# Strassen's seven products for the two down projections of a hybrid decoder layer

## The chip, the cores and the metric

One NeuronCore of one Trainium2 chip runs the whole layer in one launch. The metric is device time in microseconds, the median of several executions. In profiles, PE is TensorE's matmul, PEld its weight load, DVE is VectorE, ACT is ScalarE, POOL is GpSimd, and SP is the engine whose queue issues the DMAs.

## The reference

The kernel computes one decoder layer in float32 over 1024 tokens and 1024 channels. The change touches the two feed-forward blocks:

```python
def swiglu(x, w_gate, w_up, w_down):
    return (jax.nn.silu(x @ w_gate) * (x @ w_up)) @ w_down

x = x + 0.5 * swiglu(rmsnorm(x, ffn1_norm), ffn1_w_gate, ffn1_w_up, ffn1_w_down)   # D_FF = 2816
h = rmsnorm(x, mix_norm)
x = x + hybrid_mixer(h, ...)      # attention branch, delta-rule branch, gates, output projection
x = x + 0.5 * swiglu(rmsnorm(x, ffn2_norm), ffn2_w_gate, ffn2_w_up, ffn2_w_down)
return rmsnorm(x, final_norm)
```

The gate and up weights are 1024 x 2816, the down weights 2816 x 1024. The 2816 features are 22 tiles of 128.

## The kernel before

**Number format.** A float32 operand is split into two parts that TensorE takes at full rate: H, the value cast on ACT, and L, the rest, subtracted on DVE. A product of two split operands takes three matmuls (H·H, H·L, L·H). Weights and streamed operands come by DMA into a raw buffer (`wraw`, 128 x 1024), are cast into `wH` and subtracted into `wL` (`load_w2`, L204 and L205). `Weights` hands raw buffers and H/L pairs out in turn from several pools.

**Order.** The program is written as a sequence of tile operations. When the kernel is built, a planner gives every engine and the DMA queue a fixed order: among the instructions whose inputs and buffers it counts as ready it takes the one that stands first in the program, so that later work can be put ahead of earlier work that still waits. On the chip each queue then runs strictly in that order.

**Gate and up** (`hidden_tiles`). The features are worked on in 11 pairs of tiles, j = 0 to 10. For each j the gate half and the up half are each computed by Strassen's seven products: the input is cut into token halves and channel halves (blocks `B11`, `B21`, `T1` to `T4`, `B22`, made once and kept in SBUF), the weights into feature tile and channel halves (`seven_weights`, four POOL sums into `wS`, L346, and casts, L354 and L355). A half is 7 x 12 = 84 matmuls. The results arrive through PSUM in `ev`, `sg` and `su`. `gate_up` multiplies silu(gate) by up on POOL (L423) and stores each 128 x 512 piece to DRAM (`hd`, L424). For j = 0 and 1 (`EARLY`) two of the seven products are done earlier, while the last inputs are being made.

**Down** (`down`). Four chunks of 6, 6, 6 and 4 feature tiles; in each chunk hidden tiles (`hidH`, `hidL`, eight buffers each) and weights are loaded and split, and for every token tile t (8 of 128) and column half nh (2 of 512) one PSUM bank sums over the chunk with the hidden tile as the stationary operand (L537). DVE then adds half of the bank to x in SBUF (L539). x is loaded at the head (L552). The last chunk goes token tile by token tile, with `done(t)` after each: in the first feed-forward block the normalization of the mixer's input, in the second the final norm and the store of the output.

**Buffers.** The first feed-forward block has four raw buffers and five H/L pairs (`wp` with three, `wp1` with two), the second four raw buffers and four pairs in gate and up. `gB` is a single buffer for a gain vector, used by `load_gain`.

Of the kernel before, what the change touches and what calls it, by code (L numbers as in the profile page):

```python
# [9 lines left out]
F32 = mybir.dt.float32  # L10
# [6 lines left out]
P = 128  # L17
# [46 lines left out]
class Weights:  # L64
# [25 lines left out]
def psum(C, tag):  # L90
    return C.pp.tile([P, 512], F32, name=tag, tag=tag, bufs=BANKS[tag])
# [148 lines left out]
def load_gain(C, g):  # L240
    gB = C.tp.tile([P, D], F32, name="gB", tag="gB", bufs=1)
    C.nc.sync.dma_start(gB, bass.AP(tensor=g.tensor, offset=g.offset, ap=[[0, P], [1, D]]))
    return gB
# [177 lines left out]
def gate_up(C, out, sg, hd, i, a, eng=None):  # L421

    (eng or C.nc.gpsimd).tensor_tensor(out=out, in0=out, in1=sg, op=ALU.mult)  # L423
    C.nc.sync.dma_start(hd[:, i, a * 512:a * 512 + 512], out)  # L424


EARLY = 2
# [54 lines left out]
    return banks  # L482


def hidden_tiles(C, XB, wg, wu, hd, banks, whole):

    nc = C.nc

    def tiles(tag, bufs):
        return [[C.fp.tile([P, 512], F32, name=tag, tag=tag, bufs=bufs) for _ in range(2)] for _ in range(2)]  # L490

    for j in range(DFF // P // 2):
        rest = ((1, 1), (1, 0), (0, 1)) if j < EARLY else ((0, 0), (1, 1), (1, 0), (0, 1))

        def half(w, tag, bufs):
            early = banks.pop(0) if j < EARLY else None
            out = tiles(tag, bufs) if whole else None
            W = seven_weights(C, w, j * 256, early is not None)
            out = out or tiles(tag, bufs)
            first = j == 0 and w is wg and not whole  # L500
            seven_products(C, W, XB, out, early, PIECES if first else WHOLE, "tC" if first else "tA")
            return out

        g = half(wg, "sg", 5)
        for i, a in rest:
            nc.scalar.activation(g[i][a], g[i][a], AF.Silu)
        u = half(wu, "su", 4)
        for i, a in rest:
            gate_up(C, u[i][a], g[i][a], hd[j], i, a)


def down(C, tc, x, src, wd, hd, chunks, last, done, side):

    nc = C.nc

    def hidden(f0, n, a):
        tiles = []
        for j in range(f0 // 2, (f0 + n) // 2):
            to = [C.fp.tile([P, SLOT], F32R, name=t, tag=t, bufs=8 if not C.last else 4) for t in ("hidH", "hidL")]
            H, L = load_w2(C, hd[j][:, :, a * 512:a * 512 + 512], 2, 512, to)  # L520
            tiles += [(H[:, i], L[:, i]) for i in range(2)]
        return tiles

    def wtiles(f0, n, nh):
        W = []
        for k2 in range(0, n, 2):
            r = (f0 + k2) * P
            H, L = load_w2(C, wd[r:r + 256, nh * 512:nh * 512 + 512].rearrange("(k p) n -> p k n", p=P), 2, 512)
            W += [(H[:, 0], L[:, 0]), (H[:, 1], L[:, 1])]
        return W  # L530

    def one(t, nh, hid, W):
        ps = psum(C, "tC" if nh else "mm")
        m = slice(t % 4 * P, t % 4 * P + P)
        seq = [(hid[t // 4][k][i], W[k][w]) for k in range(len(W)) for i, w in ((0, 0), (0, 1), (1, 0))]
        for i, (h, w) in enumerate(seq):
            nc.tensor.matmul(ps, h[:, m], w, start=i == 0, stop=i == len(seq) - 1)  # L537
        xs = x[t][:, nh * 512:nh * 512 + 512]
        nc.vector.scalar_tensor_tensor(xs, ps, 0.5, xs, op0=ALU.mult, op1=ALU.add)  # L539

    f0 = 0
    C.last = False
    with tc.tile_pool(name="hid", bufs=1, side=side, reuse_waits="tile") as C.fp:
        for n in chunks:
            hid = []
            for nh in (0, 1):
                W = wtiles(f0, n, nh)
                for t in range(NT):
                    if nh == 0 and t % 4 == 0:
                        hid.append(hidden(f0, n, t // 4))  # L550
                    if f0 == nh == 0:
                        nc.sync.dma_start(x[t], src[t * P:t * P + P])  # L552
                    one(t, nh, hid, W)
            f0 += n
    C.last = True
    with tc.tile_pool(name="hidl", bufs=1, side=side, reuse_waits="tile") as C.fp:
        last()
        Ws = [wtiles(f0, 4, 0), wtiles(f0, 4, 1)]
        hid = [hidden(f0, 4, a) for a in (0, 1)]
        for t in range(NT):  # L560
            for nh in (0, 1):
                one(t, nh, hid, Ws[nh])
            done(t)

# [926 lines left out]
def ffn2(C, tc, I, out, hs):  # L1491

    nc = C.nc
    wg, wu = I["ffn2_w_gate"], I["ffn2_w_up"]
    C.XB = {}
    for i, names in enumerate((("B11", "B21"), ("T2", "T1"))):
        for q, n in enumerate(names):
            C.XB[n] = [b[i][:, q * 4:q * 4 + 4, :] for b in (C.hH, C.hL)]
    with ExitStack() as st:
        x2p = st.enter_context(tc.tile_pool(name="x2", bufs=1, side="right"))  # L1500

        x2 = dict((t, x2p.tile([P, D], F32, name=f"x2{t}")) for t in (0, 4, 1, 5, 2, 6, 3, 7))
        late, W2 = merge_out(C, tc, I, x2)
        with tc.tile_pool(name="xb2", bufs=1, reuse_waits="tile") as xb:
            for n in ("T3", "B22", "T4"):
                C.XB[n] = [xb.tile([P, 4, 512], F32R, name=n + h) for h in "HL"]
            with tc.tile_pool(name="lo", bufs=1) as lo:
                banks = early_products(C, I, late, W2, lo)
            st.close()
            with tc.tile_pool(name="f2", bufs=1, reuse_waits="tile") as C.fp:  # L1510
                C.wp.add(C.tp, 2, 0, "xs")
                hidden_tiles(C, C.XB, wg, wu, C.hd, banks, True)
    hs.close()
    with tc.tile_pool(name="x3", bufs=1, reuse_waits="tile") as xp:
        C.wp.add(xp, 0, 2)
        x = [xp.tile([P, D], F32, name=f"x{t}") for t in range(NT)]

        def done(t):
            y = xp.tile([P, D], F32, name="y", tag="xg", bufs=3)
            nc.gpsimd.tensor_tensor(out=y, in0=x[t], in1=C.gF, op=ALU.mult)  # L1520
            r = rstd(C, x[t], xp)
            nc.scalar.activation(y[:, :512], y[:, :512], AF.Copy, scale=r)  # L1522
            nc.sync.dma_start(out[t * P:t * P + P, :512], y[:, :512])
            nc.vector.tensor_scalar(y[:, 512:], y[:, 512:], r, None, op0=ALU.mult)  # L1524
            nc.sync.dma_start(out[t * P:t * P + P, 512:], y[:, 512:])

        def last():
            C.gF = load_gain(C, I["final_norm"])

        down(C, tc, x, C.x2d, I["ffn2_w_down"], C.hd, (6, 6, 6), last, done, "right")  # L1530


def layer(tc, I, out):
# [4 lines left out]
    with ExitStack() as st, ExitStack() as hs:  # L1538
# [17 lines left out]
        C.hd = [C.dp.tile([P, 2, T], F32, name=f"hd{j}") for j in range(DFF // P // 2)]  # L1556
        C.hH, C.hL = [None, None], [None, None]

        def open_h(a):
# [12 lines left out]
def ffn1(C, tc, I, open_h):  # L1572

    nc = C.nc
    with ExitStack() as st:
        C.wp.add(st.enter_context(tc.tile_pool(name="wp1", bufs=1)), 2, 2)
        C.tp = st.enter_context(tc.tile_pool(name="tp1", bufs=1))
        consts(C, I)
        with tc.tile_pool(name="xb", bufs=1) as xb:
            XB = {n: [xb.tile([P, 4, 512], F32R, name=n + h) for h in "HL"] for n in XBLOCKS if n != "T4"}  # L1580
            wg, wu = I["ffn1_w_gate"], I["ffn1_w_up"]
            with tc.tile_pool(name="s1", bufs=1) as sp:
                banks = early_tiles(C, tc, XB, I, wg, wu, C.hd, sp)
            with tc.tile_pool(name="f1", bufs=1, reuse_waits="tile") as C.fp:
                hidden_tiles(C, XB, wg, wu, C.hd, banks, False)
# [4 lines left out]
        with tc.tile_pool(name="x1", bufs=1, reuse_waits="tile") as xp:  # L1590
            x = []
            for t in range(NT):
                x.append(xp.tile([P, D], F32, name=f"x{t}"))
# [12 lines left out]
                if t > 1:  # L1606
                    late.pop(0)()

            down(C, tc, x, I["x"], I["ffn1_w_down"], C.hd, (6, 6, 6), lambda: open_h(1), done1, "left")

            C.begun = {}
            for c0, (H, L), at in ((C_QA, W[0], None), (C_KA, W[1], {5: late[1]})):
# [30 lines left out]
```

## Time and profile before

| | |
|---|---|
| median of 3 runs | 2669.09 us (2668.16 to 2672.79) |
| the profiled execution: its own time | 2673.94 us |
| its span in the trace | 2672.2 us |
| PE busy | 2581.1 us, 97%, 13007 matmuls |
| DVE busy | 1463.4 us, 55% |
| ACT busy | 1032.2 us, 39% |
| POOL busy | 468.3 us, 18% |
| DMA | 262.12 MB, mean 98 GB/s |
| granted TensorE clock, mean | 0.99 |

Busy time of PE is of pipelined matmuls, so that a stretch with 100% says that matmuls follow each other, not how long one occupies the array; the number of matmuls in a stretch says that. In the rows, the left tile is what is written, the right ones what is read; "x443" is a count; the text behind an arrow names what ended the idle time of the engine. The first feed-forward block spans about 0 to 710 us (its down from 471), the mixer to about 1980, the second block to the end (its down from about 2412).

### The profile page before, as it was taken

Reading aid. Unit: us, or ns where it says so; the run is one execution under the profiler, and the core shown is the slowest. Engines: PE = TensorE matmul, PEld = TensorE weight load, DVE = VectorE, ACT = ScalarE, POOL = GpSimd, SP = SyncE. Lnnn points to the kernel's source line nnn. Section 1 sums busy time; section 2 is a strip of 40 time slices with the busy share of each in tenths; the row PEclk is TensorE's granted clock in tenths of the full one; section 3 lists DMA queues with packets and bytes.
Section 4 is the critical chain, followed back from the end, with each engine's and each line's share of the span. In section 5 each row is a group of like instructions: output and inputs, shape, how many; then the busy total and the mean of one; then the engine's idle time right before and its main releaser. Section 6 shows DMA issues by size and latency. Waiting matters only on the chain. (4 is left out here: it accounts for less than half of the span.)

```text
span 2672.2 us, 34694 instructions
## 1 busy us (share of the span) xinstructions
PE 2581.1 (97%) x13007; PEld 2138.7 (80%) x13007; DVE 1463.4 (55%) x3276; ACT 1032.2 (39%) x1738; POOL 468.3 (18%) x378
## 2 busy tenths in 40 slices
PE   6999999999999999999999999999999999999997
PEld 5888888788788788787788888877877888887886
DVE  6444444432743547868867878445764444444326
ACT  5333333211544338445454444344433333332113
POOL 5534442000200000000000000000004445430002
PEclk9999999999999999999999999999999999999999
DMA  5323223531331222223222222367533232226311
GB/s 151 90 88 89 81 76 97 199 101 58 112 99 51 74 74 55 62 68 90 78 62 62 60 59 72 121 204 241 182 99 104 79 90 87 80 83 216 102 57 71
DMA packets 298809, 262.12 MB, mean 98 GB/s; under 512 B 39856, under 2 KB 232592, under 8 KB 298640
## 3 DMA queue, kind: packets, MB, share of 16 engines
q1 hardware_dynamic: 298640, 259.90, 31.9%
q8 instruction: 102, 1.67, 0.3%
q14 instruction: 67, 0.55, 0.1%
HBM read 195.26 MB, written 58.29 MB: 95 GB/s over the span
## 5 line engine op out<-in xcount | busy, mean ns | idle before, releaser
L229 PE MATMUL mm<-hH,wL 128*128 128x512 f32 x1072 | 442.0, 412 | 0.1
L229 PE MATMUL mm<-hL,wH 128*128 128x512 f32 x1072 | 419.8, 392 | 0.0
L229 PE MATMUL mm<-hH,wH 128*128 128x512 f32 x1072 | 418.9, 391 | 0.0
L204 ACT CAST wH<-wraw 128x1024 fp32r<-128x1024 f32 (+1 forms) x138 | 143.7, 1045 | 300.8 <-PE mm L537 123.8
L229 PEld LDWEIGHTS mm<-hL,wH 128*128 128x128 f32 x1072 | 201.5, 188 | 45.7
L229 PEld LDWEIGHTS mm<-hH,wL 128*128 128x128 f32 x1072 | 202.2, 189 | 43.7 <-issue 5.3
L205 DVE TENSOR_TENSOR wL<-wraw,wH 128x1024 fp32r<-128x1024 f32 (+1 forms) x138 | 169.7, 1231 | 112.8 <-ACT wH L204 105.6
L229 PEld LDWEIGHTS mm<-hH,wH 128*128 128x128 f32 x1072 | 202.5, 189 | 35.1
L355 DVE TENSOR_TENSOR wL<-wS,wH 128x1024 fp32r<-128x1024 f32 x88 | 126.8, 1441 | 162.1 <-ACT wH L354 161.3
L346 POOL TENSOR_TENSOR wS<-wraw 128x512 f32<-128x512 f32 x66 | 84.1, 1295 | 563.9 <-PE tA L296 322.8
L423 POOL TENSOR_TENSOR su<-su,sg 128x512 f32<-128x512 f32 x84 | 133.3, 1598 | 185.8 <-DVE su L397 161.6
L354 ACT CAST wH<-wS 128x1024 fp32r<-128x1024 f32 x88 | 92.5, 1053 | 151.0 <-PE tC L365 110.0
L393 ACT COPY ev<-mm 128x512 f32<-128x512 f32 (+1 forms) x118 | 68.5, 581 | 201.7 <-PE mm L365 201.7
L537 PE MATMUL mm<-wH,hidH 128*128 128x512 f32 x352 | 137.8, 392 | 3.0 <-DVE x L539 1.9
L537 PE MATMUL mm<-wH,hidL 128*128 128x512 f32 x352 | 137.5, 391 | 2.6 <-DVE hidL L205 2.6
L537 PE MATMUL tC<-wH,hidH 128*128 128x512 f32 x352 | 137.4, 391 | 1.9 <-ACT wH L204 1.9
L537 PE MATMUL mm<-wL,hidH 128*128 128x512 f32 x352 | 137.1, 390 | 1.3 <-DVE wL L205 1.3
L537 PE MATMUL tC<-wL,hidH 128*128 128x512 f32 x352 | 137.6, 391 | 0.5 <-DVE wL L205 0.5
L537 PE MATMUL tC<-wH,hidL 128*128 128x512 f32 x352 | 137.7, 391 | 0.0
L914 POOL MEMSET xp<- 128x3 f32 x24 | 2.4, 100 | 653.9 <-PE tA L775 250.9
L539 DVE SCALAR_TENSOR_TENSOR x<-mm,x 128x512 f32<-128x512 f32 x64 | 44.0, 689 | 105.2 <-PE mm L537 104.3
L539 DVE SCALAR_TENSOR_TENSOR x<-tC,x 128x512 f32<-128x512 f32 x64 | 44.0, 688 | 86.6 <-PE tC L537 86.5
(432 smaller groups left out, 6029.0 us busy)
## 6 DMA issues: line engine op xcount, KB each, us to landing
wraw<-in_w_in_dram SPq DMA_DIRECT2D x64, 512.0 KB, 4.1
wraw<-in_ffn_w_gate_dram SPq DMA_DIRECT2D x48, 512.0 KB, 4.6
hd<-su SPq DMA_DIRECT2D x84, 256.0 KB, 3.2
wraw<-in_ffn_w_down_dram SPq DMA_DIRECT2D x33, 512.0 KB, 4.3
wraw<-hd SPq DMA_DIRECT2D x33, 512.0 KB, 4.7
wraw<-in_ffn_w_up_dram SPq DMA_DIRECT2D x26, 512.0 KB, 4.7
xs<-in_ffn_w_up_dram SPq DMA_DIRECT2D x22, 512.0 KB, 3.9
wraw<-in_w_branch_b_dram SPq DMA_DIRECT2D x16, 512.0 KB, 4.5
```

The costliest lines, as they stand in the source:

```text
L204: nc.scalar.copy(H[:, :width], raw[:, :width])
L205: (nc.gpsimd if C.pool_split else nc.vector).tensor_tensor(out=L[:, :width], in0=raw[:, :width], in1=H[:, :width].bitcast(F32), op=ALU.sub ...
L229: ins = nc.tensor.matmul(ps, w[:, k, :], x[:, k, :], start=k == 0 and i == 0, stop=k == kt - 1 and i == 2)
L346: nc.gpsimd.tensor_tensor(out=out, in0=p, in1=q, op=op)
L354: nc.scalar.copy(H[:, :n], srcs)
L355: eng.tensor_tensor(out=L[:, :n], in0=srcs, in1=H[:, :n].bitcast(F32), op=ALU.subtract)
L393: nc.scalar.copy(v[:, s], ps[:, s])
L423: (eng or C.nc.gpsimd).tensor_tensor(out=out, in0=out, in1=sg, op=ALU.mult)
L537: nc.tensor.matmul(ps, h[:, m], w, start=i == 0, stop=i == len(seq) - 1)
L539: nc.vector.scalar_tensor_tensor(xs, ps, 0.5, xs, op0=ALU.mult, op1=ALU.add)
L914: nc.gpsimd.memset(xp[:, 0:3], 0.0)
```

## The change

Both down projections are cut as Strassen products. Tiles 0 to 3 (j below `EARLY`) are done as before; tiles 4 to 21 (j = 2 to 10) are cut three ways into halves: even and odd feature tiles, token halves, column halves. Nine tiles of each parity remain.

- Behind the gate half of each such j, `down_blocks` loads two 128 x 1024 row tiles of the down weights into `gB` and a new single buffer `wY`, makes the four weight differences T1 to T4 with four POOL operations in place, and stores them to DRAM (`tb`).
- Behind `gate_up` of each such j, `hidden_blocks` makes four sums of the hidden blocks on POOL, over buffers of `sg` and `su` that are no longer needed, and stores seven blocks of 128 x 512 (`ab`) where the four pieces of `hd` were stored.
- `down` runs the seven products one after the other in the order of `DOWN`. Each streams its hidden block and its weight block from DRAM in five chunks of 2, 2, 2, 2, 1 tiles, and its four token tiles sum in four open banks; two sets of four banks alternate, and three products go on in banks whose earlier sum is still there. After each product four adds bring the banks to x.
- The four plain tiles follow, token tile by token tile with `done(t)`.
- The hidden buffers shrink from eight to four and are placed first in the freed memory, where `B11` and `B21` lay; x comes behind them. The first block has one pair less (`wp1`: 2, 1), the second block's down two raw buffers more.

```diff
-    C.nc.sync.dma_start(hd[:, i, a * 512:a * 512 + 512], out)
+    if hd is not None:
+        C.nc.sync.dma_start(hd[:, i, a * 512:a * 512 + 512], out)
...
+def slot(n):
+    n -= EARLY
+    return n // 2, n % 2
+
+def hidden_blocks(C, u, g, n):
+    (a11, a21), (a12, a22) = u
+    s1, s2, s3, s4 = g[1][1], g[0][0], a21, g[1][0]
+    for out, p, q, op in ((s1, a21, a22, ALU.add), (s3, a11, a21, ALU.subtract), (s2, s1, a11, ALU.subtract), (s4, a12, s2, ALU.subtract)):
+        C.nc.gpsimd.tensor_tensor(out=out, in0=p, in1=q, op=op)
+    c, i = slot(n)
+    for name, v in (("A11", a11), ("A12", a12), ("A22", a22), ("S1", s1), ("S3", s3), ("S2", s2), ("S4", s4)):
+        C.nc.sync.dma_start(C.ab[name][c][:, i, :], v)
+
+def down_blocks(C, wd, n):
+    nc = C.nc
+    X, Y = [pool.tile([P, SLOT], F32, name=tag, tag=tag, bufs=1) for pool, tag in ((C.tp, "gB"), (C.fp, "wY"))]
+    for i, r in enumerate((X, Y)):
+        nc.sync.dma_start(r, wd[(2 * n + i) * P:(2 * n + i + 1) * P])
+    lo, hi = slice(0, 512), slice(512, 1024)
+    for out, p, q in ((X[:, lo], X[:, hi], X[:, lo]), (X[:, hi], Y[:, hi], X[:, hi]), (Y[:, hi], Y[:, hi], X[:, lo]), (Y[:, lo], Y[:, lo], Y[:, hi])):
+        nc.gpsimd.tensor_tensor(out=out, in0=p, in1=q, op=ALU.subtract)
+    c, i = slot(n)
+    for k, r in enumerate((X, Y)):
+        nc.sync.dma_start(C.tb[c][:, i, k, :], r)
...
         g = half(wg, "sg", 5)
+        if j >= EARLY:
+            down_blocks(C, wd, j)
         for i, a in rest:
             nc.scalar.activation(g[i][a], g[i][a], AF.Silu)
         u = half(wu, "su", 4)
         for i, a in rest:
-            gate_up(C, u[i][a], g[i][a], hd[j], i, a)
+            gate_up(C, u[i][a], g[i][a], hd[j] if j < EARLY else None, i, a)
+        if j >= EARLY:
+            hidden_blocks(C, u, g, j)
...
+DOWN = (("A11", "B11", 0, True, (0, 0)), ("A12", "B21", 1, True, (0, 0)), ("S2", "T2", 0, False, (0, 1)), ("S1", "T1", 1, True, (1, 1)),
+        ("S3", "T3", 0, False, (1, 1)), ("S4", "B22", 1, False, (0, 1)), ("A22", "T4", 0, False, (1, 0)))
...
+def down(C, x, src, wd, hd, done):
...
+    def hidden(v, n):
+        return load_w2(C, v, n, 512, [C.fp.tile([P, SLOT], F32R, name=t, tag=t, bufs=4) for t in ("hidH", "hidL")])
...
+    def mms(ps, m, hid, W, n, first, stop, more=False):
+        seq = [(hid[i][:, k], W[w][:, k]) for k in range(n) for i, w in ((0, 0), (0, 1), (1, 0))]
+        for i, (h, w) in enumerate(seq):
+            nc.tensor.matmul(ps, h[:, m], w, start=first and i == 0, stop=stop and i == len(seq) - 1, skip_group_check=more)
+
+    banks = [[psum(C, tag) for tag in tags for _ in range(2)] for tags in (("mm", "tM"), ("tA", "tC"))]
+    loaded = False
+    for a, b, z, begin, (half, nh) in DOWN:
+        if begin and z and loaded:
+            banks[1] = [psum(C, tag) for tag in ("tA", "tC") for _ in range(2)]
+        for c, v in enumerate(C.ab[a]):
+            n = v.shape[1]
+            A, B = hidden(v, n), weights(b, c, n)
+            for t in range(4):
+                mms(banks[z][t], slice(t * P, t * P + P), A, B, n, begin and c == 0, c == len(C.ab[a]) - 1, not begin)
+            if not loaded and c > 0:
+                for t in range(c * 2 - 2, c * 2):
+                    nc.sync.dma_start(x[t], src[t * P:t * P + P])
+        loaded = True
+        for t in range(4):
+            add(half * 4 + t, nh, banks[z][t])
+    Ws = [[weights_plain(C, wd, c, nh) for c in range(EARLY)] for nh in (0, 1)]
+    hid = [[hidden(hd[c][:, :, q * 512:q * 512 + 512], 2) for c in range(EARLY)] for q in (0, 1)]
+    for t in range(NT):
+        for nh in (0, 1):
+            ps = psum(C, "mm" if nh else "tC")
+            for c in range(EARLY):
+                mms(ps, slice(t % 4 * P, t % 4 * P + P), hid[t // 4][c], Ws[nh][c], 2, c == 0, c == EARLY - 1)
+            add(t, nh, ps)
+        done(t)
...
-        C.wp.add(xp, 0, 2)
+        C.wp.add(xp, 2, 2)
...
-        C.wp.add(st.enter_context(tc.tile_pool(name="wp1", bufs=1)), 2, 2)
+        C.wp.add(st.enter_context(tc.tile_pool(name="wp1", bufs=1)), 2, 1)
```

More of the change, by code (lines that the diff above doesn't have):

```diff
@@ L482, in early_tiles, with hidden_tiles @@
     return banks
-def hidden_tiles(C, XB, wg, wu, hd, banks, whole):
+def slot(n):
[20 more added lines that the diff above has]
+        nc.sync.dma_start(C.tb[c][:, i, k, :], r)
+def hidden_tiles(C, XB, wg, wu, wd, hd, banks, whole):
     nc = C.nc
@@ L508, in hidden_tiles @@
         for i, a in rest:
-            gate_up(C, u[i][a], g[i][a], hd[j], i, a)
-def down(C, tc, x, src, wd, hd, chunks, last, done, side):
-    nc = C.nc
[L516 to L537, printed above, removed]
+            gate_up(C, u[i][a], g[i][a], hd[j] if j < EARLY else None, i, a)
@@ new lines, in hidden_tiles, with weights, add @@
+        if j >= EARLY:
+            hidden_blocks(C, u, g, j)
+DOWN = (("A11", "B11", 0, True, (0, 0)), ("A12", "B21", 1, True, (0, 0)), ("S2", "T2", 0, False, (0, 1)), ("S1", "T1", 1, True, (1, 1)),
+        ("S3", "T3", 0, False, (1, 1)), ("S4", "B22", 1, False, (0, 1)), ("A22", "T4", 0, False, (1, 0)))
+WHERE = {"T1": (0, 0), "T3": (0, 1), "T4": (1, 0), "T2": (1, 1)}
+def down(C, x, src, wd, hd, done):
+    nc = C.nc
+    def hidden(v, n):
+        return load_w2(C, v, n, 512, [C.fp.tile([P, SLOT], F32R, name=t, tag=t, bufs=4) for t in ("hidH", "hidL")])
+    def weights(name, c, n):
+        if name in WHERE:
+            k, q = WHERE[name]
+            v = C.tb[c][:, :n, k, q * 512:q * 512 + 512]
+        else:
+            i, q = int(name[1]) - 1, int(name[2]) - 1
+            j = EARLY + 2 * c
+            v = wd.rearrange("(j i p) n -> i p j n", i=2, p=P)[i][:, j:j + n, q * 512:q * 512 + 512]
+        return load_w2(C, v, n, 512)
+    def add(t, nh, ps):
@@ L538, in one @@
         xs = x[t][:, nh * 512:nh * 512 + 512]
         nc.vector.scalar_tensor_tensor(xs, ps, 0.5, xs, op0=ALU.mult, op1=ALU.add)
[L541 to L563, printed above, removed]
+    def mms(ps, m, hid, W, n, first, stop, more=False):
+        seq = [(hid[i][:, k], W[w][:, k]) for k in range(n) for i, w in ((0, 0), (0, 1), (1, 0))]
+        for i, (h, w) in enumerate(seq):
+            nc.tensor.matmul(ps, h[:, m], w, start=first and i == 0, stop=stop and i == len(seq) - 1, skip_group_check=more)
@@ new lines, in down, with weights_plain @@
+    Ws = [[weights_plain(C, wd, c, nh) for c in range(EARLY)] for nh in (0, 1)]
[7 more added lines that the diff above has]
+        done(t)
+def weights_plain(C, wd, c, nh):
+    return load_w2(C, wd[c * 256:c * 256 + 256, nh * 512:nh * 512 + 512].rearrange("(k p) n -> p k n", p=P), 2, 512)
@@ L1511, in ffn2 @@
                 C.wp.add(C.tp, 2, 0, "xs")
-                hidden_tiles(C, C.XB, wg, wu, C.hd, banks, True)
+                hidden_tiles(C, C.XB, wg, wu, I["ffn2_w_down"], C.hd, banks, True)
     hs.close()
-    with tc.tile_pool(name="x3", bufs=1, reuse_waits="tile") as xp:
-        C.wp.add(xp, 0, 2)
+    with tc.tile_pool(name="hid", bufs=1, side="right", reuse_waits="tile") as C.fp, tc.tile_pool(name="x3", bufs=1, reuse_waits="tile") as xp:
+        C.wp.add(xp, 2, 2)
         x = [xp.tile([P, D], F32, name=f"x{t}") for t in range(NT)]
@@ L1525, in done @@
             nc.sync.dma_start(out[t * P:t * P + P, 512:], y[:, 512:])
-        def last():
-            C.gF = load_gain(C, I["final_norm"])
-        down(C, tc, x, C.x2d, I["ffn2_w_down"], C.hd, (6, 6, 6), last, done, "right")
+        C.gF = load_gain(C, I["final_norm"])
+        down(C, x, C.x2d, I["ffn2_w_down"], C.hd, done)
 def layer(tc, I, out):
@@ L1555, in layer @@
         C.ud = [C.dp.tile([32, 1024], F32, name=f"ud{f}") for f in range(2)]
-        C.hd = [C.dp.tile([P, 2, T], F32, name=f"hd{j}") for j in range(DFF // P // 2)]
+        C.hd = [C.dp.tile([P, 2, T], F32, name=f"hd{j}") for j in range(EARLY)]
+        sizes = [min(2, DFF // P // 2 - j) for j in range(EARLY, DFF // P // 2, 2)]
+        C.ab = {b: [C.dp.tile([P, n, 512], F32, name=f"{b}_{c}") for c, n in enumerate(sizes)] for b, *_ in DOWN}
+        C.tb = [C.dp.tile([P, n, 2, SLOT], F32, name=f"tb{c}") for c, n in enumerate(sizes)]
         C.hH, C.hL = [None, None], [None, None]
@@ L1584, in ffn1 @@
             with tc.tile_pool(name="f1", bufs=1, reuse_waits="tile") as C.fp:
-                hidden_tiles(C, XB, wg, wu, C.hd, banks, False)
+                hidden_tiles(C, XB, wg, wu, I["ffn1_w_down"], C.hd, banks, False)
             C.xt4.__exit__(None, None, None)
@@ L1589, in ffn1 @@
         gm = load_gain(C, I["mix_norm"])
-        with tc.tile_pool(name="x1", bufs=1, reuse_waits="tile") as xp:
+        with tc.tile_pool(name="hid", bufs=1, reuse_waits="tile") as C.fp, tc.tile_pool(name="x1", bufs=1, reuse_waits="tile") as xp:
             x = []
@@ L1607, in done1 @@
                     late.pop(0)()
-            down(C, tc, x, I["x"], I["ffn1_w_down"], C.hd, (6, 6, 6), lambda: open_h(1), done1, "left")
+            open_h(1)
+            down(C, x, I["x"], I["ffn1_w_down"], C.hd, done1)
             C.begun = {}
```

## The prediction

> **What bounds the kernel now.** I read first the page's shares of the span, then the windows of the two stages that the change touches, then the rows of the down projections, and last the queues around them.
>
> ```profile
> span 2672.2 us, 34694 instructions
> PE 2581.1 (97%) x13007; PEld 2138.7 (80%) x13007; DVE 1463.4 (55%) x3276; ACT 1032.2 (39%) x1738; POOL 468.3 (18%) x378
> ...
> 200.00:300.00 100.00, 100.00 (x443) 82.81 (x442) 40.85 (x43) 35.23 (x48) 48.45 (x35) 1.00 0.28 82
> 500.00:550.00 50.00, 50.00 (x222) 41.42 (x221) 22.20 (x24) 12.44 (x12) 0.00 (x0) 1.00 0.39 126
> ...
> 2100.00:2200.00 100.00, 100.00 (x443) 82.81 (x442) 44.34 (x44) 35.12 (x48) 45.41 (x31) 1.00 0.29 86
> ```
>
> The window rows give PE, PEld, DVE, ACT and POOL busy time with counts, then the granted clock, the DMA share and GB/s. TensorE is the bound: in gate and up (200 to 300, 2100 to 2200) and in down (500 to 550) it issues without a gap at full clock, 443 matmuls in 100 us, so 0.2257 us each. The 389 to 390 ns that single rows show is a pipelined length, not a price; the step between starts is. DVE, ACT and DMA are below half, POOL at 45 to 48% in gate and up and idle in down.
>
> ```profile
> L537 PE MATMUL mm<-wH,hidH x352: 387/389/518, 471.5 to 2655.1; 128*128 128x512 f32 x176
> ...
> 470.00:475.00 5.00, 3.48 (x16) 2.42 (x14) 3.29 (x3) 0.91 (x1) 3.31 (x2) 1.00 0.66 195
> 480.00:485.00 5.00, 5.00 (x24) 4.14 (x23) 0.00 (x0) 0.83 (x1) 0.00 (x0) 1.00 1.05 411
> 485.00:490.00 5.00, 3.11 (x15) 2.24 (x14) 3.65 (x4) 1.28 (x2) 0.00 (x0) 1.00 1.02 404
> ...
> 2415.00:2420.00 5.00, 3.68 (x17) 2.80 (x16) 2.79 (x3) 1.05 (x1) 2.15 (x1) 1.00 0.80 246
> 2420.00:2425.00 5.00, 3.27 (x15) 2.38 (x13) 2.36 (x2) 2.88 (x3) 0.00 (x0) 1.00 0.90 306
> 2425.00:2430.00 5.00, 4.26 (x11) 3.05 (x12) 2.62 (x3) 0.16 (x1) 0.00 (x0) 0.67 1.02 417
> ```
>
> Six such groups of 352 (two banks, three operand pairs) are 2112 matmuls, 1056 for each down. Gaps stand mainly at their heads: the first and third window shown lose 1.52 and 1.89 us, the three from 2415 lose 1.32, 1.73 and 0.74 and, at clock 0.67 (11 matmuls where 23 fit), about 2 us more, together some 10 us. DMA reaches 411 GB/s there.
>
> **The matmuls removed.** The plain product takes 22 feature tiles x 3 x 8 token tiles x 2 column halves = 1056. Afterwards seven products of half the size each way take 9 tiles x 3 x 4 token tiles = 108 each, 756, and the four plain tiles 4 x 3 x 8 x 2 = 192: 948. So 108 go in each down, 216 in all, all of them at places where PE has no gap: 216 x 0.2257 = **-48.8 us**. Gate and up keep their matmuls.
>
> **The stream in down.** Each product is cut in five chunks (2, 2, 2, 2, 1 feature tiles of a block). A full chunk is 24 matmuls, 5.42 us, and needs two 512 KB loads, two ACT casts and two DVE subtractions.
>
> ```profile
> L205 DVE TENSOR_TENSOR hidL<-wraw,hidH 128x1024 fp32r<-128x1024 f32 x16 | 19.5, 1224 | 16.6 <-ACT hidH L204 16.2
> L204 ACT CAST hidH<-wraw 128x1024 fp32r<-128x1024 f32 x16 | 16.7, 1052 | 49.7 <-PE tC L537 26.4 <-DMA wraw<-hd 23.3
> L539 DVE SCALAR_TENSOR_TENSOR x<-mm,x 128x512 f32<-128x512 f32 x64 | 44.0, 689 | 105.2 <-PE mm L537 104.3
> ...
> hd<-su SPq DMA_DIRECT2D x84, 256.0 KB, 3.2
> wraw<-in_ffn_w_down_dram SPq DMA_DIRECT2D x33, 512.0 KB, 4.3
> wraw<-hd SPq DMA_DIRECT2D x33, 512.0 KB, 4.7
> ...
> DMA to landing us min/median/max: 2.3/3.5/8.3
> ```
>
> ACT 2.10 and DVE 2.45 us of 5.42; bytes 1.05 MB in 5.42 us = 194 GB/s, against the 411 seen. A raw buffer turns over in 4.7 + 1.05 + 1.22 = 7.0 us; ffn1 has four and a chunk takes two, so chunks can follow every 3.5 us. The four adds of a product (2.8 us) have 24.4 us, one product on the other banks, before theirs are written again. Cover in every case, price 0. If landing rose to 8.5 us, (8.5 + 2.3)/2 = 5.4 and the cover is gone. In the first product x adds 4.2 MB: 8.9 MB less the 2.1 MB that four raw buffers hold beforehand, in 24.4 us, is 279 GB/s, still under 411.
>
> **The heads of down.** The hidden buffers shrink from eight pairs to four and now lie where B11 and B21 lay, whose last use is the second of the last seven products, five products (13.5 us) before the end; casts can run ahead of the switch. Against that stand seven stores of the last tile, four of them after its last product, in front of loads on SP's queue. Bounds: -10 us (all the gaps above gone) to +10 (doubled). I take 0, nearest to the rows as they are.
>
> **Gate and up, steady.** Nine tiles of each FFN get eight more POOL subtractions or additions of 128x512, two 512 KB loads, two 512 KB stores, and seven 256 KB stores in place of four.
>
> ```profile
> 2089.84 2.54 POOL L346 TENSOR_TENSOR wS<-wraw 128x512 f32<-128x512 f32 x2 [11.98 <-DVE wL L355]
> 2092.34 1.30 POOL L346 TENSOR_TENSOR wS<-wS,wraw 128x512 f32<-128x512 f32 x1
> 2093.72 1.29 POOL L346 TENSOR_TENSOR wS<-wraw,wS 128x512 f32<-128x512 f32 x1
> 2094.97 2.27 POOL L423 TENSOR_TENSOR su<-su,sg 128x512 f32<-128x512 f32 x1
> 2102.64 1.30 POOL L423 TENSOR_TENSOR su<-su,sg 128x512 f32<-128x512 f32 x1 [5.41 <-DVE su L397]
> 2104.69 1.67 POOL L423 TENSOR_TENSOR su<-su,sg 128x512 f32<-128x512 f32 x1 [0.75 <-DVE su L397]
> 2107.47 1.28 POOL L423 TENSOR_TENSOR su<-su,sg 128x512 f32<-128x512 f32 x1 [1.11 <-issue]
> 2109.91 2.54 POOL L346 TENSOR_TENSOR wS<-xs 128x512 f32<-128x512 f32 x2 [1.16 <-DVE wL L355]
> ...
> 2127.93 2.54 POOL L346 TENSOR_TENSOR wS<-wraw 128x512 f32<-128x512 f32 x2 [11.98 <-DVE wL L355]
> ```
>
> One tile takes 38.09 us (2089.84 to 2127.93), and POOL is idle 5.41 + 0.75 + 1.11 + 1.16 + 11.98 = 20.4 of it. Eight operations at 1.29 are 10.3 us; at 1.8, a value between the plain and the longest here, 14.4. Both fit. The block sums of the hidden tile wait for the last gate_up and stand ahead of the next sums wS: they need 4 x 1.29 = 5.2 of the 11.98 us of idle, so those sums start late by up to some 6 us. Who waits then is ACT's cast of wS:
>
> ```profile
> 2201.64 0.39 PE L365 MATMUL mm<-hH,wH 128*128 128x512 f32 x1
> 2206.59 1.30 POOL L346 TENSOR_TENSOR wS<-wS,wraw 128x512 f32<-128x512 f32 x1
> 2212.57 1.05 ACT L354 CAST wH<-wS 128x1024 fp32r<-128x1024 f32 x1 [1.98 <-PE tC L365]
> ```
>
> The cast comes 4.7 us after the sum ends (2207.89) because PE frees its buffer only then, and its weights are used in the third product of the next half, 2201.64 + (84 + 24) x 0.2257 = 2226.0, 13 us later. A delay of 6 us puts ACT back by 1.3 us, and nothing on PE. ffn1 falls from five weight pairs to four, which is what ffn2 has, and ffn2's windows are full. SP issues 15 DMAs for 8, 0.4 us each, of 38; DMA goes from 86 to about 150 GB/s. Price 0, with bounds in the rivals.
>
> ```profile
> L346 POOL TENSOR_TENSOR wS<-xs,wS 128x512 f32<-128x512 f32 x9 | 19.4, 2157 | 0.7
> ```
>
> This group is the sum that in the other half takes 1.29 (2093.72): where a DVE subtraction runs beside it, it takes 0.87 us more.
>
> The Trainium skill, page "SBUF — State Buffer", section "Who interferes with whom", says that a VectorE instruction with two SBUF inputs and a GpSimd instruction reading SBUF exclude each other, the later one waiting in full. By that rule the tile would need 20 POOL operations x 1.29 = 25.8 plus six wL of 1.22 and two of 0.69 = 8.7, together 34.5 of 38.1 us, so the sum would be the same 2628 while POOL's work is spread evenly, and worse where it is bunched. The trace agrees with the waiting, 2.16 for 1.29.
>
> **Gate and up, the beginning.** The differences of the down weights depend on no matmul, only on two single buffers, and the queues are planned: what is ready is put forward.
>
> ```profile
> 52.03 0.38 SPq L242 DMA_DIRECT2D gB<-in_mix_norm_dram  x1
> ...
> 65.00:70.00 5.00, 1.80 (x7) 1.51 (x8) 2.69 (x4) 2.61 (x3) 3.11 (x3) 0.81 0.08 20
> ...
> 70.60 2.92 POOL L346 TENSOR_TENSOR wS<-wraw 128x512 f32<-128x512 f32 x2 [2.42 <-DVE wL L355]
> ...
> 313.42 2.54 POOL L346 TENSOR_TENSOR wS<-wraw 128x512 f32<-128x512 f32 x2 [5.57 <-DVE wL L355]
> 315.92 1.29 POOL L346 TENSOR_TENSOR wS<-wS,wraw 128x512 f32<-128x512 f32 x1
> 317.29 1.29 POOL L346 TENSOR_TENSOR wS<-wraw,wS 128x512 f32<-128x512 f32 x1
> 318.54 5.23 POOL L423 TENSOR_TENSOR su<-su,sg 128x512 f32<-128x512 f32 x3
> ...
> 314.57 0.69 DVE L397 TENSOR_TENSOR su<-ev,tC 128x512 f32<-128x512 f32 x1 [1.23 <-ACT ev L393]
> ```
>
> The mixer's gain is loaded into gB 420 us before the down that precedes its use. And four sums stand before a gate_up of an earlier tile whose input was ready at 315.26, 1.9 us after the sums began: the plan took three of them for less than 2 us, at most 0.65 each, half of what they take. So the first differences will come while tiles 0 and 1 are still computed, where sums run just in time and PE has gaps (65 to 70): 4 x 1.29 = 5.2 in a gap of 2.42, **+2.8 us** in each FFN, +5.6. Bounds 0 (they come later) and 10.4 (no gap to use).
>
> **The end of ffn1's down.** The four plain weight pairs fill all four pairs, so the first mixer weights are cast and subtracted only when one comes free, four us before the end: 0 to 1.05 + 1.22 = 2.3. The normalization keeps ACT and DVE busy there; I take **+2.3**.
>
> **Sum.** 2673.94 of the profiled execution (its span and 1.7 us around it) - 48.8 + 5.6 + 2.3 = 2633.0; the median lies 4.85 lower, so **2628 us**, its own range 2613 to 2645.
>
> **The rivals.**
> A, POOL's order held up (slower). A difference needs its load: three operations, a store and a load, 3.9 + 3.2 + 4.3 = 11.4 us a tile at the least; planned with half-length operations, 3 x 0.65 + 7.5 = 9.5 or less, nine in 85 us, 2.2 tile periods. If POOL stands still through each of these chains, nine take 103 us. Those 2.2 periods have 2.2 x (20.4 - 5.2) = 33 us of idle; that leaves 69 us of delay, less the 13 us of lead 56 on PE per FFN: -48.8 + 112 = 2732. It turns slower from 24.4 us per FFN, which is when the nine chains stand in 4.3 periods or fewer. For it: the run-ahead and the half-length plan. Against it: other work fits into the waits; POOL's own work in those 2.2 periods, 9 x 5.2 + 2.2 x 20.7 = 92 us of 84, is 8 late, under the 13.
> B, the same only in part: chains that stand in six periods leave 103 - 91 = 12, which the lead covers unless subtractions on DVE stretch the 36 operations of the differences: half of them by 0.87 is 16 us more, 12 + 16 - 13 = 15 per FFN, 2669.1 - 48.8 + 30 + 2.3 = 2653.
> C, down bound by its stream: landing at the 8.3 us of the longest row plus 2 us gives 6.3 us per chunk, +0.9 x 63 chunk lengths = +57: 2686. Against it 194 of 411 GB/s.
> D, the products are not saved: were a matmul that goes on in an open bank longer by a tenth, 1512 of them would give back 34 us: 2663. Against: gate and up accumulate third and seventh products into open banks in the same way, in windows that are full.
>
> **How the numbers follow.** Forecast 0.62, B 0.19, A 0.11, C 0.05, D and others 0.03. Range 2613 (heads gone, -10, and some of the start's cost) to 2668: it leaves out A, C and a little above and below. What this kernel's runs can tell from no change is 0.2%, 5.3 us. Faster 0.81 (forecast and B), slower 0.14 (A, most of C, D), same 0.05.
>
> **What would show it.** 12,791 matmuls; down at 222 per 50 us and about 214 us long, at near 190 GB/s; gate and up at 443 per 100 us with POOL at 70%, more at its start. Wrong if windows between 100 and 250 or between 2040 and 2190 fall under 430 per 100 us with PE waiting for casts of wS, or if SP and ACT wait in down for landings above 8 us.

## The result and the profile after

The changed kernel takes 2699.89 us (median of 5 runs, 2697.95 to 2706.74), the kernel before 2669.64 beside it (2668.16 to 2673.3): ratio 1.0115, interval 1.01 to 1.0129. It is 1.1% slower, where 2628 was forecast and 2668 was the upper end.

The page of the kernel after, its span and first part:

```profile
span 2695.9 us, 35044 instructions
...
PE 2549.1 (95%) x12791; PEld 2110.8 (78%) x12791; DVE 1504.0 (56%) x3304; ACT 1085.6 (40%) x1806; POOL 693.7 (26%) x522
```

The 216 matmuls are gone, 12,791 for 13,007, and PE is busy 32 us less (2581.1 before); yet the span is 23.7 us longer. So PE stands still about 56 us more than it did. The windows say where (PE, PEld, DVE, ACT and POOL busy with counts, granted clock, DMA share, GB/s):

```profile
100.00:150.00 50.00, 50.00 (x222) 41.19 (x220) 18.45 (x20) 14.70 (x20) 34.47 (x25) 1.00 0.58 195
150.00:200.00 50.00, 39.78 (x163) 32.22 (x163) 15.88 (x16) 13.04 (x18) 38.28 (x29) 0.90 0.72 236
200.00:250.00 50.00, 39.37 (x168) 32.19 (x167) 17.42 (x17) 14.78 (x20) 36.16 (x26) 0.90 0.41 137
250.00:300.00 50.00, 50.00 (x222) 41.40 (x221) 21.84 (x23) 18.65 (x26) 30.24 (x21) 1.00 0.33 100
500.00:550.00 50.00, 41.97 (x162) 32.98 (x161) 25.04 (x23) 14.25 (x16) 11.26 (x6) 0.90 0.70 248
550.00:600.00 50.00, 50.00 (x223) 41.40 (x222) 27.07 (x30) 18.52 (x20) 0.00 (x0) 1.00 0.66 209
2100.00:2150.00 50.00, 39.75 (x163) 31.96 (x162) 16.62 (x16) 13.04 (x18) 37.82 (x29) 0.90 0.69 226
2150.00:2200.00 50.00, 38.96 (x161) 31.64 (x160) 16.02 (x16) 13.24 (x18) 34.67 (x25) 0.86 0.44 142
```

The same place is hit in both FFNs: two windows of 50 us lose 54 to 61 of some 222 matmuls each, and from 250 on (2200 in the second block) gate and up is full again. Down itself (550 to 600) runs without a gap, and its head (500 to 550) loses 60 matmuls. By the starts of each stage's first and last matmuls, of which the lines of ffn1's down are, before (one row) and after (two):

```profile
L537 PE MATMUL tC<-wH,hidL x176: 388/389/397, 509.5 to 723.1; 128*128 128x512 f32 x176
```

```profile
L579 PE MATMUL mm<-wH,hidH x104: 387/389/740, 502.2 to 735.2; 128*128 128x512 f32 x104
...
L579 PE MATMUL mm<-wH,hidL x104: 389/389/628, 504.3 to 735.7; 128*128 128x512 f32 x104
```

| us | before | after | difference |
|---|---|---|---|
| ffn1: gate and up, to the first matmul of down | 471.5 | 502.2 | +30.7 |
| ffn1: down, first to last matmul | 251.6 | 233.5 | -18.1 |
| last matmul of down to the mixer's first into `mm` (L229) | 14.5 | 17.0 | +2.5 |
| mixer from there to ffn2's first matmul on L365 | 1233.5 | 1229.2 | -4.3 |
| ffn2: gate and up, to the first matmul of down | 440.2 | 474.7 | +34.5 |
| ffn2: down, to its last matmul | 246.9 | 225.9 | -21.0 |

The mixer's own lines are unchanged; what makes its 4.3 us is not known.

The chain behind the gate-and-up loss can be read from both ends. The waits of ACT (40 to 500 us), before and then after, and of PE after (0 to 800 us), columns total, times, longest:

```profile
ACT wH L354 <- POOL wS L346: 5.1, 4, 2.6
...
ACT wH L354 <- POOL wS L346: 69.7, 16, 15.2
...
PE tC L365 <- DVE sg L397: 24.6, 4, 10.6
```

In the kernel before, PE has no wait for L397 at all in this stretch.

And the timelines around the longest of them (start, length, instruction, idle before it and its releaser): POOL, then ACT, then DVE.

```profile
189.38 1.28 POOL L423 TENSOR_TENSOR su<-su,sg 128x512 f32<-128x512 f32 x1
194.06 1.28 POOL L511 TENSOR_TENSOR gB<-gB 128x512 f32<-128x512 f32 x1 [3.40 <-DMA gB<-in_ffn_w_down_dram]
195.31 1.29 POOL L423 TENSOR_TENSOR su<-su,sg 128x512 f32<-128x512 f32 x1
196.55 1.29 POOL L511 TENSOR_TENSOR gB<-wY,gB 128x512 f32<-128x512 f32 x1
...
201.89 1.26 POOL L497 TENSOR_TENSOR sg<-su 128x512 f32<-128x512 f32 x1
...
205.67 1.26 POOL L346 TENSOR_TENSOR wS<-wraw 128x512 f32<-128x512 f32 x1
...
208.11 1.26 POOL L346 TENSOR_TENSOR wS<-wS,wraw 128x512 f32<-128x512 f32 x1
...
193.61 0.59 ACT L393 COPY ev<-mm 128x512 f32<-128x512 f32 x1 [1.29 <-PE mm L365]
209.40 1.04 ACT L354 CAST wH<-wS 128x1024 fp32r<-128x1024 f32 x1 [15.21 <-POOL wS L346]
210.35 0.58 ACT L393 COPY ev<-mm 128x512 f32<-128x512 f32 x1
...
211.62 0.68 DVE L397 TENSOR_TENSOR sg<-ev,tC 128x512 f32<-128x512 f32 x1
```

The sums wS (L346) stand in POOL's queue behind the last differences (L511), gate_ups (L423) and block sums (L497). ACT waits 15.21 us for them in front of its cast, and with it waits the copy of a finished bank (L393) that stands behind the cast and needs nothing from POOL. DVE's sum of that bank (L397) comes after the copy, and PE, whose bank tC it empties, stands still 10.6 us. PE thus waits for a bank, not for weights.

### The profile page after: what moved, and what is told of

It is laid out like the page before. It is cut to its first block, busy times and chain, and to the rows that moved or that the text cites. A ratio compares the mean times of both kernels' runs of the same rounds, so it can differ in the third digit from the quotient of the medians.

```text
span 2695.9 us, 35044 instructions
## 1 busy us (share of the span) xinstructions
PE 2549.1 (95%) x12791; PEld 2110.8 (78%) x12791; DVE 1504.0 (56%) x3304; ACT 1085.6 (40%) x1806; POOL 693.7 (26%) x522
## 5 line engine op out<-in xcount | busy, mean ns | idle before, releaser
L229 PE MATMUL mm<-hH,wL 128*128 128x512 f32 x1072 | 442.6, 413 | 0.1
L229 PE MATMUL mm<-hL,wH 128*128 128x512 f32 x1072 | 420.3, 392 | 0.0
L229 PE MATMUL mm<-hH,wH 128*128 128x512 f32 x1072 | 419.5, 391 | 0.0
L205 DVE TENSOR_TENSOR wL<-wraw,wH 128x1024 fp32r<-128x1024 f32 (+2 forms) x171 | 205.1, 1200 | 121.7 <-ACT wH L204 114.4
L204 ACT CAST wH<-wraw 128x1024 fp32r<-128x1024 f32 (+2 forms) x171 | 173.5, 1018 | 187.7 <-PE mm L229 76.7
L229 PEld LDWEIGHTS mm<-hL,wH 128*128 128x128 f32 x1072 | 201.8, 188 | 45.6
L229 PEld LDWEIGHTS mm<-hH,wL 128*128 128x128 f32 x1072 | 202.7, 189 | 44.0 <-issue 5.3
L229 PEld LDWEIGHTS mm<-hH,wH 128*128 128x128 f32 x1072 | 202.9, 189 | 35.1
L423 POOL TENSOR_TENSOR su<-su,sg 128x512 f32<-128x512 f32 x84 | 130.9, 1561 | 141.9 <-DVE su L397 122.3
L393 ACT COPY ev<-mm 128x512 f32<-128x512 f32 (+1 forms) x118 | 68.4, 580 | 170.3 <-PE mm L365 170.3
L365 PE MATMUL tC<-B22H,wH 128*128 128x512 f32 (+1 forms) x180 | 75.3, 418 | 52.5 <-DVE sg L397 45.8
L204 ACT CAST hidH<-wraw 128x1024 fp32r<-128x1024 f32 (+1 forms) x64 | 62.2, 979 | 151.0 <-PE tM L579 54.2
L346 POOL TENSOR_TENSOR wS<-wraw 128x512 f32<-128x512 f32 x66 | 90.9, 1393 | 105.7 <-DVE wL L355 91.4
L511 POOL TENSOR_TENSOR gB<-gB 128x512 f32<-128x512 f32 x18 | 25.3, 1403 | 360.0 <-DVE x L318 313.0
L205 DVE TENSOR_TENSOR hidL<-wraw,hidH 128x1024 fp32r<-128x1024 f32 (+1 forms) x64 | 77.3, 1212 | 69.8 <-ACT hidH L204 69.7
L579 PE MATMUL mm<-wH,hidH 128*128 128x512 f32 x208 | 82.9, 400 | 12.7 <-ACT wH L204 12.7
L365 PEld LDWEIGHTS tC<-B22H,wH 128*128 128x128 f32 x180 | 36.7, 204 | 63.5 <-DVE sg L397 48.3
L579 PE MATMUL mm<-wL,hidH 128*128 128x512 f32 x208 | 83.2, 400 | 0.5 <-DVE wL L205 0.5
L354 ACT CAST wH<-wraw 128x512 fp32r<-128x512 f32 (+1 forms) x60 | 49.0, 816 | 86.0 <-PE tM L365 48.4
```

Source lines behind the costliest of these rows:

```text
L204: nc.scalar.copy(H[:, :width], raw[:, :width])
L205: (nc.gpsimd if C.pool_split else nc.vector).tensor_tensor(out=L[:, :width], in0=raw[:, :width], in1=H[:, :width].bitcast(F32), op=ALU.sub ...
L229: ins = nc.tensor.matmul(ps, w[:, k, :], x[:, k, :], start=k == 0 and i == 0, stop=k == kt - 1 and i == 2)
L346: nc.gpsimd.tensor_tensor(out=out, in0=p, in1=q, op=op)
L354: nc.scalar.copy(H[:, :n], srcs)
L365: C.nc.tensor.matmul(ps[:, s], w[:, k, :], x[:, k, s], start=first and k == 0 and i == 0, stop=k == 3 and i == 2, skip_group_check=not first)
```

## The experiments

The times below are medians; each ratio is against the kernel before on the same chip, with its interval.

**The order alone.** The loads and stores of a tile's differences are kept behind the gate load, and its subtractions behind the seven weights' sums, of the same tile; nothing is left out or added.

```
-        nc.sync.dma_start(r, cols(w, c0 + i * P))
+        C.raw_dma = nc.sync.dma_start(r, cols(w, c0 + i * P))
...
-        nc.gpsimd.tensor_tensor(out=out, in0=p, in1=q, op=op)
+        C.sum_op = nc.gpsimd.tensor_tensor(out=out, in0=p, in1=q, op=op)
...
-            down_blocks(C, wd, j)
+            with C.tc.issue_after(C.raw_dma.ins), C.tc.issue_after(C.sum_op.ins):
+                down_blocks(C, wd, j)
```

> Theory (order): the weight differences run ahead of their tiles, stand in POOL's queue in front of sums that PE needs, and POOL waits in order for their loads. Here the loads of the differences of tile j are issued behind the raw loads of its gate half, and their POOL operations behind the sums of its gate half; the work and the bytes are those of the changed kernel. Theory: gate and up goes back to its length before, first down matmul near 472 to 476 us instead of 502, the median 2632 to 2645. Rival throughput (POOL and DVE have too much to do for 38 us a tile, whatever the order): the stalls only spread, 2690 to 2700. Rival traffic (the added DMA delays weight loads): same bytes, 2680 to 2700.

Measured 2629.79 us, ratio 0.9842 (0.9825 to 0.9859): 70 us below the change as it was made, with the same arithmetic. Its windows:

```profile
150.00:200.00 50.00, 50.00 (x223) 41.39 (x222) 21.81 (x20) 17.35 (x23) 42.07 (x29) 1.00 0.40 132
...
2150.00:2200.00 50.00, 50.00 (x222) 41.41 (x221) 22.26 (x20) 16.76 (x22) 42.07 (x28) 1.00 0.41 133
```

Gate and up takes 470.8 and 442.1 us, as before (471.5 and 440.2), with POOL busier than in the disturbed windows, 42.07 for 38.28 us. So in the changed kernel it is the order of the differences that costs, not their number.

**No differences.** `down_blocks` does nothing; the products with T blocks read plain weights.

> Leaves out the weight differences, their loads, POOL operations and stores; the products T1 to T4 read plain weight blocks instead. The sums of the hidden blocks stay. Theory (order): as with the differences spread out, within 4 us, 2630 to 2642, first down matmul near 472. Rival hidden sums (the four sums behind gate_up are what delays): as the changed kernel, 2690 to 2700.

2628.8, ratio 0.9844 (0.9823 to 0.9865). The block sums of the hidden tiles and their stores, which remain, cost nothing in gate and up (439.0 in ffn2); that rival falls. Nor do differences in their own tile cost more than none at all.

**Their transfers alone.** Loads and stores run ahead as in the change; the four POOL operations are left out.

```
-        nc.gpsimd.tensor_tensor(out=out, in0=p, in1=q, op=ALU.subtract)
+        pass
```

> Leaves out only the four POOL operations of each weight difference: the loads into gB and wY and the stores behind them stay, and run ahead. Theory (order): POOL has nothing of them in its queue, so gate and up is back at its length, 2632 to 2648, first down matmul 471 to 478. Rival traffic: the delay stays, first down matmul 490 to 502, 2680 to 2700.

2629.78, ratio 0.9848 (0.9824 to 0.9871), with gate and up at 472.1 and 437.0 us. DMA and SP's queue fall as the cause: the early transfers are free when POOL doesn't take part.

**The differences alone.** The kernel before, with the differences computed and stored but not read, and the fewer weight pairs of the change; the down projections stay as before.

> The kernel before with the weight differences alone added (made, stored and read by nobody) and one H/L pair less in the first block, which their buffer needs; down as before. Theory (order): gate and up takes 24 to 31 us more in each block, first down matmul near 496 to 502, in all 2718 to 2732. Rival hidden sums: 2670 to 2680, first down matmul near 473.

2731.37, ratio 1.0228 (1.0208 to 1.0249), +60.6 us. Two windows and the wait:

```profile
150.00:200.00 50.00, 40.36 (x166) 32.83 (x167) 16.57 (x16) 13.05 (x18) 36.44 (x28) 0.90 0.72 234
200.00:250.00 50.00, 42.07 (x175) 34.34 (x174) 18.83 (x19) 16.05 (x22) 24.49 (x18) 0.90 0.36 110
...
PE tC L365 <- DVE sg L397: 22.2, 4, 8.5
```

Gate and up is 30.1 and 31.5 us late. The loss comes with the differences by themselves (and one weight pair fewer, which the spread kernel has too); the down stage has no part in it.

**Two operations of four.** The last two of a tile's four subtractions are left out, the run-ahead is kept.

> The changed kernel with the differences running ahead, but the last two of their four POOL operations left out (T1 and T4 are then plain weights): the chain of load, operations, store, load stays, POOL's operation time falls from 5.2 to 2.6 us a tile. If POOL's waits for the loads make the delay: the gate and up of each block still takes 20 to 28 us more than before, 2680 to 2695. If POOL's operation time makes it, with a lead of some 13 us before PE feels it: 0 to 10 us a block, 2635 to 2655.

2660.77, ratio 0.997 (0.9958 to 0.9981), between the two expected ranges, so neither expectation held. Gate and up is 13.7 and 13.0 us late where the whole has 30.7 and 34.5. Nine tiles less two operations of 1.29 to 1.50 us are 23 to 27 us of POOL's time, and 17 and 21.5 of it came back on PE. What is left stands beside waits of POOL (50 to 260 us) that stop its queue:

```profile
POOL gB L511 <- DMA gB<-in_ffn_w_down_dram: 35.6, 7, 8.6
```

So the length of POOL's operations carries a large part, and the rest stands beside the stops for loads. Fewer operations also shorten the chain (57.2 to 180.3 us, for 56.6 to 200.6 in the changed kernel), so the two are not parted by this run.

**POOL's order alone.** Only the subtractions are kept behind the sums of their tile; SP's queue is free to run ahead.

> As e1_spread, but only POOL's operations are tied (behind the sums of the gate half of their tile); the loads into gB and wY may come as early as their buffers allow. Theory (order in POOL's queue): as e1_spread, 2625 to 2636, first down matmul 470 to 475. Rival (the early loads themselves hold SP's queue): between e1_spread and the changed kernel, above 2645.

2632.61, ratio 0.9852 (0.9819 to 0.9885); first matmul of down at 469.4. The order in POOL's queue is what matters. The two single buffers keep the loads of this run close to those of the first (163.10 us for 167.47), so it says little of loads that run far ahead; for those the transfers alone speak. That SP's order alone would do nothing was not tried.

**Spread, but twice the operations.** As the first, with each subtraction issued twice, 24 POOL operations per tile.

> As e1_spread, with each of the four operations of a difference carried out twice in place (the T blocks then hold other values): 24 POOL operations a tile for 20, some 31 to 38 us of 38. Theory (order and a lead of some 13 us): POOL is nearly full but in step, 0 to 6 us a block, 2630 to 2642. Rival throughput (POOL with DVE is what fills first): at 24 x 1.6 us = 38 us it no longer fits, 5 us a tile, +45 us a block, 2690 to 2720.

2681.64, ratio 1.0032 (1.0016 to 1.0048), some 50 us above the first. My expectation of 2630 to 2642 missed; the rival, throughput, had the kind of loss right and was too high, with +45 us a block where +24 and +23 came. Its windows, and its waits on PE, ACT and POOL (200 to 500 us):

```profile
200.00:250.00 50.00, 47.50 (x210) 39.00 (x209) 20.35 (x21) 16.22 (x22) 44.15 (x31) 1.00 0.43 140
250.00:300.00 50.00, 47.45 (x210) 38.93 (x209) 20.79 (x20) 16.27 (x23) 44.20 (x31) 1.00 0.49 158
...
PE tC L365 <- DVE sg L397: 17.8, 7, 2.6
...
ACT wH L354 <- POOL wS L346: 49.8, 7, 7.1
...
POOL wS L346 <- DVE wL L355: 29.1, 6, 4.9
```

This loss is another: not one burst, but some 2.5 us in every tile, whose period grows from 38.1 to 40.97 us. POOL, DVE and ACT wait for each other in a ring (wL frees wS, wS releases the cast, the cast stands before the bank's copy), and with POOL 88% busy the ring no longer closes in 38.1 us; this is read off the three waits, and no run changed the ring itself. So 20 operations fit and 24 do not: the margin of the change is thin even in good order. In the first experiment (250 to 440 us) groups of POOL and the window show why:

```profile
L346 POOL TENSOR_TENSOR wS<-wS,wraw 128x512 f32<-128x512 f32 x10 | 13.0, 1296 | 0.0
L511 POOL TENSOR_TENSOR gB<-gB 128x512 f32<-128x512 f32 x5 | 11.3, 2269 | 0.0
L511 POOL TENSOR_TENSOR wY<-wY 128x512 f32<-128x512 f32 x5 | 10.8, 2152 | 0.4
...
250.00:440.00 190.00, 190.00 (x840) 157.31 (x839) 84.66 (x81) 67.35 (x90) 151.93 (x101) 1.00 0.49 159
```

Equal shapes take 1.30 or 2.27 us; POOL's 101 operations keep it busy 151.93 of 190 us, 1.50 each and 80%, where I had 1.29 and 70%. The long ones stand beside DVE's subtractions. In the kernel before, the same window has 60 operations in 85.03 us, 1.42 each, so 1.29 was too short for the rows at hand as well.

**The heads of down.** What is left in the spread kernel is the stall at the first matmuls of down. Its SP queue and PE wait there:

```profile
476.23 0.33 SPq L500 DMA_DIRECT2D S<-sg  x1
478.46 0.33 SPq L500 DMA_DIRECT2D S<-su  x1
480.69 1.69 SPq L500 DMA_DIRECT2D S<-sg  x2
482.47 0.39 SPq L203 DMA_DIRECT2D wraw<-in_ffn_w_down_dram  x1
...
PE mm L580 <- ACT wH L204: 5.2, 1, 5.2
```

SP issues the last tile's four block-sum stores in order, each when POOL has made its sum, and the weight load behind them waits 11 us for sums it doesn't need. Two edits, each on top of the spread order: x loaded later, one tile a chunk; and these four stores issued from POOL's queue.

```
-            if not loaded and c > 0:
-                for t in range(c * 2 - 2, c * 2):
+            if a in ("A11", "A12") and c > 0:
+                t = c - 1 + (4 if a == "A12" else 0)
+                with C.tc.issue_after(C.load.ins):
...
-        C.nc.sync.dma_start(C.ab[name][c][:, i, :], v)
+        (C.nc.gpsimd if n == DFF // P // 2 - 1 and name[0] == "S" else C.nc.sync).dma_start(C.ab[name][c][:, i, :], v)
```

> The differences tied to their tile as in e1_spread; besides, the eight loads of x at the head of down are issued one behind each chunk's loads in the first two products, instead of two behind each chunk of the first. Theory stores (SP waits for POOL's last hidden sums with four stores, and the weight load that PE needs stands behind them): little changes, the stall of 5 and 7.6 us at the heads stays, within 5 us of e1_spread. Rival x (the x loads fill the DMA engines when chunks are due): the stall goes, 12 to 20 us faster than e1_spread.

> As e1_spread, and the four stores of the last tile's hidden sums are issued from POOL's own queue, behind the sums, instead of from SP. Theory stores: the weight load that came at 482.5 us is issued near 475, the stall of 5.2 us falls under 1 and the clock is kept, 5 to 8 us in each block, 2614 to 2622. Rival x: no change, 2626 to 2634.

> Both edits of the head on top of e1_spread. Theory stores: as the stores alone or a little better, 2610 to 2622. Rival x: as the x loads alone. If both delay, the sum of both, 2605 to 2615.

Later x: 2626.54, ratio 0.9836 (0.9814 to 0.9858), 3 us by the medians and under 2 by the ratios, which their intervals don't tell from nothing; the stalls are still 5.2 and 6.0. The four stores on POOL: 2617.43, ratio 0.9803 (0.9786 to 0.9819), 12 us by the medians and 10 by the ratios. Its SP and POOL queues:

```profile
470.60 0.38 SPq L203 DMA_DIRECT2D wraw<-in_ffn_w_down_dram  x1
...
478.36 0.74 POOL L500 DMA_DIRECT2D S<-sg  x1
```

The load is issued at 470.60 for 482.47, and the stall of ffn1 is gone; the mixer's first matmul into `mm` comes 239.2 us after the first of down, for 249.5. In ffn2 a stall of 4.4 us stays, and its down is only 3.1 us shorter. Both edits: 2615.42 us (2613.78 to 2616.51), ratio 0.9794 (0.9779 to 0.9808), the lowest median here, though not clear of the stores alone; it is 2.1% below the one before and 84 below the change as it was made. One stall of 6.2 us stays at ffn2's head, where DVE's wL is late. There DVE stands idle in front of a subtraction, and the trace names a load of x as what ended it:

```profile
2390.34 0.69 DVE L205 TENSOR_TENSOR wL<-xs,wH 128x512 fp32r<-128x512 f32 x1 [12.52 <-DMA x<-x2d]
```

In this block four loads of x are still issued within 3.1 us (2377.62 to 2380.73). Why a subtraction that doesn't read x waits for one is open.

## Why the prediction was wrong

**The step that failed** is the term "Gate and up, the beginning", +2.8 us per FFN. It measured +30.7 and +34.5, 60 of the 72 us between 2628 and 2699.89. The mechanism was named, as rival A with a chance of 0.11: the differences are put forward, planned at half length, and hold POOL's order up. Its turning point was nine chains in 4.3 tile periods or fewer; they stood between 56.6 and 200.6 us, 3.8 periods of 38.1 (in ffn2 4.0, 1999.6 to 2153.7). With these periods the rival's own sum, 103 less 15.2 a period and 13 of lead, gives 32 and 29. That this is near the measured size is luck: the 13 in it is not the lead that counted (below), and its 103 us has POOL standing still through every chain, where it waited 28 and 37 us for the differences' loads and worked most of the rest. So the run-ahead that A describes was right, though no run tested that half-length planning makes it, and two arguments that set A aside were wrong:

- "POOL's own work is 8 late, under the 13." That sum took every operation at 1.29 and no stop. POOL waited 26.2 us in ffn1 for the differences' loads, with everything in its queue behind; I wrote that "other work fits into the waits", which a queue in order allows only if the other work stands ahead. The window 150 to 200 shows POOL 38.28 of 50 us busy while PE starves: late, not full.

```profile
POOL gB L511 <- DMA gB<-in_ffn_w_down_dram: 26.2, 6, 8.4
```

- The 13 us of lead. It was worked out for the weights that the sum feeds, and those were indeed not what PE waited for. The late cast stands in ACT's queue in front of a copy out of PSUM, and that copy's bank is wanted back much sooner. Between the product that the copy empties and the one that needs `tC`, PE has one product of 12 matmuls (198.85 to 201.57 us), 2.7 us; less the copy's 0.58 and the sum's 0.68 that is a lead of some 1.4 us, by estimate, for 13. The lead that counts is that of the first thing queued behind the waiting instruction.

**Right:** the matmuls removed (12,791; 222 to 223 per 50 us in down, so -48.8); the stream in down at price 0 (209 GB/s for 194, windows full); gate and up, steady, at price 0, though on 80% of POOL and not 70. For the last the spread kernel speaks, full from 100 us to the end of gate and up; in the changed kernel the differences are done by 201 us, so its full windows from 250 on don't test it.

**Right in size, by luck in part:** the end of ffn1's down, +2.3 for +2.5 measured. The prediction has PE wait for the mixer's first weights; what PE waits for (460 to 760 us) is the normalization of the last tokens, whose steps stand on ACT and DVE behind the casts and subtractions of those weights:

```profile
PE tA L266 <- ACT xg L260: 3.0, 1, 3.0
```

**The spread kernel** is what the prediction described, and at 2629.79 it lies 2 us from the forecast, because errors cancel: its start cost about 1 for 5.6 (470.8 and 442.1 us of gate and up for 471.5 and 440.2), and its heads 3.6 and 3.0 for 0 (down is 20.8 and 21.4 us shorter).

**The heads of down** were taken at 0, within -10 to +10. Down got 18.1 and 21.0 shorter for 24.4, so they cost 6.3 and 3.4 more than before. The four stores "in front of loads on SP's queue" were named there and not priced. In the kernel after the row is ACT's wait, then two windows:

```profile
517.91 1.04 ACT L204 CAST wH<-wraw 128x1024 fp32r<-128x1024 f32 x1 [16.53 <-DMA wraw<-in_ffn_w_down_dram]
...
515.00:520.00 5.00, 0.74 (x1) 0.24 (x1) 1.01 (x1) 1.04 (x1) 0.00 (x0) 0.91 0.98 334
520.00:525.00 5.00, 4.73 (x11) 3.77 (x12) 1.44 (x2) 1.05 (x1) 0.00 (x0) 0.50 1.04 408
```

PE issues one matmul in 5 us and then runs at clock 0.50, 11 for 22 in the next five, so a stall of 4.9 us costs some 7.4, an estimate with 11 missing matmuls at 0.2257. The Trainium skill, page "TensorE: Matmul & The Clock Gate", section "Part 1: The HAM clock gate", says that the clock falls to half after an idle window of about 3.4 us; the trace agrees, with 0.50 behind this gap.

**The profiled runs** differ by 24.0 us (2697.95 and 2673.94), the medians by 30.25: the execution profiled before was slower than the five that give the median, that after was the fastest of its runs. The table adds up to the former, within a microsecond.

**Rivals C and D** (down bound by its stream, products not saved) are excluded by the full window 550 to 600 (four of the seven products, not three, go on in banks with an earlier sum, and the third of all stands in this window). D's 2663, which the prediction counts among the slower outcomes, would have been 6 us faster than the kernel before. B's 2653 had the same cause as A, at six periods.

## What to carry to other kernels

When work that depends on nothing is added, a planner that fixes the order of queues by estimated lengths can put it at the front, as here; read the estimate off an existing queue, and tie the new work to the step it belongs to, which here was worth 70 us. Price a delayed instruction by the first thing queued behind it, not by the use of its own result, and count a wait inside a queue as a stop of all that follows. Before an engine off the critical path gets more work, take its operations at their measured mean beside their neighbours, not at the shortest row.

## What the hardware showed that I had not expected

An issue of a store costs POOL 0.53 to 0.74 us of its own time here, and was still worth 10 to 12 us, because it took a wait out of SP's queue. And POOL's operations of 128x512, 1.29 us at the shortest, took 1.50 us on average in the spread kernel's gate and up, with DVE beside them; at a busy share of 88% POOL no longer kept up with the tiles.
